# A hybrid encoder layer on one core: unit matrix ahead of the gram tiles, A queries ahead of A values, and other buffers for half of the output weight

## The chip, the core and the metric

The kernel runs on one core of a Trainium2 chip. The core has five engines with queues of their own: TensorE (PE, matrix products into PSUM), VectorE (DVE), ScalarE (ACT), GpSimd (POOL) and SyncE (SP, which here issues nearly all the DMAs). An engine works through its queue in order: an instruction that waits holds all that stand behind it on the same engine. The metric is the device time of one execution in microseconds; smaller is better. Matrix products are made of three matmuls with operands split into a high and a low part, so that the result is close to float32.

## What is computed

One layer of a streaming encoder on x of 1024 rows (tokens) by 1024 columns. Cut to its core:

```python
h = rms_norm(x, pre_norm_g)
proj = h @ w_in + b_in                       # 1024 x 3724, split by columns:
# a_q a_k a_v a_i a_f a_z | b_x b_z | c_r c_k c_v c_w c_a c_z | d_q d_k d_v d_f d_z
y_a = head_rms_norm(mlstm_chunkwise(silu(conv(a_q, a_k)), a_v, a_i, a_f)) * silu(a_z)
y_b = multiscale_pool(b_x) * silu(b_z)
y_c = rwkv7_time_mix(c_r, c_k, c_v, c_w, c_a, ...) * silu(c_z)
y_d = forgetting_attention(rms_norm(d_q), rms_norm(d_k), d_v, d_f) * silu(d_z)
y = concat(y_a, y_b, y_c, y_d) @ w_out
x = x + rms_norm(y, post_norm_g)
x = x + rms_norm(memory_cross_attention(rms_norm(x), rms_norm(mem), wq, wkv, wo))
```

Group C is a recurrence over tokens, S_t = S_{t-1}(diag(w_t) - kk^T (a*kk)) + v^T k. The kernel turns it into chunks of 64 tokens. Inside a chunk the recurrence is a triangular system, whose matrix has to be inverted; between chunks a state is passed on.

## The kernel before, in words

**Stages.** (1) The memory is normalised and its keys and values are computed; x is normalised and transposed. (2) The projections of group C (`cproj`) and their preparation (`cnorm`, `csplit`, `cprep`). (3) The gram tiles (`cgram`), the inverses (`cinv`, `tinv`) and the chain over 16 chunks (`cchain`). (4) Group A (`mpre`, `mlstm`) and group B. (5) Group D (`flog`, `ftr`, `fav`, `fin`) with the output projection (`wout`, `outproj`) beside it. (6) Cross attention.

**Order.** From stage 2 to the end of stage 5 PE's order is the order of the program text (`manual_schedule`). The queues of the other engines are put in order ahead of time by a planner, which takes instructions by their priority and by when it reckons that their inputs and buffers are ready; `high_priority` moves an instruction forward, `issue_after` holds it behind another one of the same engine. The orders are fixed when the kernel is built.

**Fillers.** The other projections are generators in a list, `fillers`. `fill(n)` takes n steps from the first of them, and when it is used up goes on to the next. One step of `tgemm` is three matmuls of 512 columns; `ngemm_q`, which the values use, counts a step as 0.5, with three matmuls of 268 or 256 columns. A generator writes its eviction when it is asked for the step after its last, so the fill after the 32nd step is the one in which the eviction of a `tgemm` of 32 steps enters the program. `ngemm_q` goes over the eight row blocks in groups of 2, 2 and 4 and keeps its four weight pieces to the last group; `tgemm` gives each piece back when its steps are done. The weight pieces go through the buffers "wr" (raw, two), "wh" and "wl" (four each). Results are put into "zu" (four buffers) on the way to DRAM. `rgemm` (the queries and keys) may carry norms of its results (`square`, `norm1`), which are put in after a number of filler steps.

**Preparation.** After the four `cnorm`, `fill(9)`, the tanh and split of the low-rank columns under `issue_after` of the last instruction named `act["cproj"]` so far, and `fill(5)` (L962 to L966). Then four groups of `cprep`, each followed by `fill(13)` and the second half of the group before it (L968 to L975), then `fill(4)`.

**Inverses.** `cgram` (L565) multiplies keys with queries of each chunk pair on PE; DVE masks one half into `bq`, ACT copies the other half back and POOL masks it (L581 to L585); sixteen DMAs write 32 by 32 blocks to the DRAM tile dN. `cinv` (L595) loads them with one DMA on ACT's queue, writes a unit matrix into `Tn` with two memsets on POOL (L599, L600) and inverts in 31 steps of two DVE instructions each (L604, L606). Result and transpose go to DRAM, and `tinv` (L611) reads them back in another layout; its first products on PE are L630. Between the loads and these products stands `fill(NI)`, NI = 46. The buffers "n4" (four of them) hold Nt and Tn, then the tiles of `tinv`, later the gate rows (`gaterows`, two of them) and the inputs of the convolution (`aconv`).

**Chain.** Each `cchain` takes three fills of two steps. After chunk c one piece of `gaterows` follows from c = 3 on, and one of `aconv` from c = 8 on. What is left of the fillers follows the chain (L1017).

**Output weight.** `wout(q)` (L1311) loads the 128 by 512 pieces k = 0 to 7 of the columns' half q, casts them on ACT and subtracts on POOL (k = 1, 4, 7) or DVE. Even pieces land in "wr", odd ones in "zu". `wout(0)` is called at the third step of group D (g = 2), `wout(1)` at the fifth, after which the buffers' pools are closed and the gain vector "gb" of the output projection is loaded into their room. The D gate (`zgemm(O_DZ, 3, True)`) is the filler at that time; its results go through "zu" too, and `tload` reads them from the DRAM tile zT for `tgate` and `fin`.

Of the kernel before, what the change touches and what calls it, by code (L numbers as in the profile page):

```python
# [36 lines left out]
def tile_trunk(ctx: ExitStack, tc: tile.TileContext, a, out, dbg=None):  # L37
# [63 lines left out]
    def wtile(kind, shape):  # L101
        dt = F32 if kind == "wr" else F32R
        n = wcount[kind]
        wcount[kind] += 1
        if cur["wp0"] is not None:
            a1, a0 = cur["wp"].tags[kind], cur["wp0"].tags[kind]
            if n % (a1 + a0) >= a1:
                return cur["wp0"](kind, shape, dt)
        return cur["wp"](kind, shape, dt)
# [285 lines left out]
    def fill(n):  # L395

        while n > 0 and fillers:
            try:
                w = next(fillers[0]) or 1
            except StopIteration:  # L400
                fillers.pop(0)
                continue
            n -= w
            for d in after:
                d[0] -= w
            for d in [d for d in after if d[0] <= 0]:
                after.remove(d)
                d[1]()
# [183 lines left out]
                    SY.dma_start(dN[q0:q0 + 8].rearrange("q s t -> s q t"),  # L592
                                 bq[r0:r0 + 32, cp * 2 - 2:cp * 2 + 2, :, r0:r0 + 32].rearrange("p c j t -> p (c j) t"))

    def cinv():  # L595
        Nt = cc("n4", [128, 32, 32])
        SC.dma_start(Nt, dN)
        Tn = cc("n4", [128, 32, 32])
        G.memset(Tn, 0.0)  # L599
        G.memset(Tn.rearrange("p a b -> p (a b)")[:, ::33], 1.0)  # L600
        for j in range(31):
            m = 31 - j
            pr = cc("pr", [128, m, j + 1])
            V.tensor_tensor(pr, Nt[:, j, j + 1:32][:, :, None].to_broadcast([128, m, j + 1]),  # L604
                            Tn[:, j, 0:j + 1][:, None, :].to_broadcast([128, m, j + 1]), op=ALU.mult)
            V.tensor_tensor(Tn[:, j + 1:32, 0:j + 1], Tn[:, j + 1:32, 0:j + 1], pr, op=ALU.add)  # L606
        V.tensor_copy(Nt, Tn.rearrange("p a b -> p b a"))
        SY.dma_start(dTt, Nt)
        SY.dma_start(dTn, Tn)
# [45 lines left out]
            SC.copy(SV[c - 1][0:64, 1::2, :], p[0:64, :, 64:128])  # L655

    FA, FB, FC = 2, 2, 2
    NI = 46
    BN = {}

    def cbk(c):
# [84 lines left out]
    def vgemm(wd, bias, c0, n, dst):  # L746
        ng = n - 256
        b = cm("bias", [128, 268])
        SY.dma_start(b[:, 0:n], bcast(bias[c0:c0 + n], n))

        zz = []

        def ev(i, p):
            if i % 2 == 0:
                zz.append(cur["stg"]("zu", [128, 2, 256]))
            z = zz[-1][:, i % 2, :]
            SC.copy(z, p[:, 0:256])
            if ng:
                SC.copy(gates[:, i, :], p[:, 256:n])  # L759
            if i % 2:  # L760
                V.tensor_tensor(zz[-1], zz[-1], b[:, None, 0:256].to_broadcast([128, 2, 256]), op=ALU.add)
                if ng:
                    g = gates[:, i - 1:i + 1, :]
                    V.tensor_tensor(g, g, b[:, None, 256:n].to_broadcast([128, 2, ng]), op=ALU.add)
                SY.dma_start(dst[(i - 1) * 128:(i + 1) * 128, :].rearrange("(a p) c -> p a c", a=2), zz[-1])
        yield from ngemm_q(wd, c0, n, hact, ev)
# [33 lines left out]
    def rgemm(c0, b0, r0, gcl=None, lag=None):  # L800
        us = []

        def put(t):
            c, hf = divmod(t, 2)
            SY.dma_start(rT[r0 + c * 128:r0 + (c + 1) * 128, hf * 512:(hf + 1) * 512], us[t])

        def square(t):
            sq = cur["stg"]("zt", [128, 512])
            SC.activation(sq, us[t], AF.Square)
            parts = [[cc(t_, [128, 256], F32R) for t_ in tags] for tags in (("bv", "yc"), ("ysb", "w"))]  # L810
            for q in range(2):
                qs = slice(q * 256, (q + 1) * 256)
                split_evac(parts[0][q], parts[1][q], sq[:, qs])
            defer(lag[t], lambda: norm(t, parts))

        def norm(t, parts):
            with tc.issue_after(act["ln"].ins):
                norm1(t, parts)

        def norm1(t, parts):  # L820
            p = ps("sm", [128, 512])
            for q in range(2):
                qs = slice(q * 256, (q + 1) * 256)
                T.matmul(p[:, qs], onesr, parts[0][q], start=True, stop=False)
                T.matmul(p[:, qs], onesr, parts[1][q], start=False, stop=True)
            if t < 3:
                square(t + 1)
            SC.activation(p, p, AF.Ln, bias=eps_n, scale=1.0 / 64)
            SC.activation(p, p, AF.Exp, scale=-0.5)
            V.scalar_tensor_tensor(us[t], us[t], col(gcl), p, op0=ALU.mult, op1=ALU.mult)  # L830
            put(t)

        def ev(c, p):
            for hf in range(2):
                u = cur["stg"]("zu", [128, 512])
                us.append(u)
                SC.activation(u, p[hf], AF.Identity, bias=col(b0 + c))
                if gcl is None:
                    put(2 * c + hf)
            if gcl is not None and c == 0:  # L840
                square(0)
        yield from tgemm(c0, 2, ev)
# [110 lines left out]
    with tc.manual_schedule(engines={PE}):  # L953
        run(cproj(6, 1))
        run(cproj(2, 2))
        fillers += [cproj(0, 2), cproj(4, 2), rgemm(O_DQ, 66, 0, 46, (7, 6, 6, 6))]
        gs = [cnorm(hf, j) for hf in range(2) for j in range(2)]
        for g in gs:
            next(g)
            fill(6)  # L960
            run(g)
        fill(9)  # L962
        with tc.issue_after(act["cnorm"].ins), tc.issue_after(act["cproj"].ins):
            SC.activation(shifted[6][0:64, :], shifted[6][0:64, :], AF.Tanh)
            csplit(0)
        fill(5)  # L966
        gs = [cprep(hf, j) for hf in range(2) for j in range(2)]
        for n, g in enumerate(gs):  # L968
            with tc.issue_after(act["cnorm"].ins):
                next(g)  # L970
            if g is gs[-1]:
                act["ln"] = tc.keep_in_program_order(SC.preload_act_table_set("natural_log_exp_and_others"))
            fill(13)
            if n:
                run(gs[n - 1])  # L975
        cur["vsplit"] = True
        fill(4)
        run(gs[-1])
        c1.close()
        fillers += [rgemm(O_DK, 68, 256, 47, (6, 6, 5, 5)), vgemm(a["w_av"], a["b_av"][0], 0, 268, avd), rgemm(O_AQ, 0, 512)]  # L980
        cc = Pool("cc", {"bq": 2, "n4": 4, "pr": 1, "t11": 1, "sv": 3, "ik": 2, "bn": 2, "w": 1, "uu": 1,
                         "bv": 1, "yc": 1, "ysb": 1})
        for _ in range(2):
            t = cc("ik", [128, 4, 64])
            for x in range(2):
                V.tensor_copy(t[PH[x], x::2, :], ident[PH[x], None, x * 64:(x + 1) * 64].to_broadcast([64, 2, 64]))
            IK.append(t)
        cprop(0)
        V.memset(SV[0][0:64, 0::2, :], 0.0)
        V.memset(SV[0][64:128, 1::2, :], 0.0)  # L990
        cgram(0, 1)
        cgram(1, 1)
        cinv()
        ti = [tinv(0), tinv(1)]
        next(ti[0])
        cur["vsplit"] = False
        fill(NI)
        next(ti[0])
        fill(4)
        run(ti[0])  # L1000
        fill(3)
        fillers += [rgemm(O_AK, 2, 768), vgemm(w_in, b_in, O_DV, 256, dvd)]
        gr, ac = gaterows(), aconv()
        tc.cur_priority = 150000
        cprop(1)
        cbk(0)
        for c in range(16):
            cchain(c)
            if c < 3:
                next(ti[1], None)  # L1010
            if c >= 3:
                next(gr, None)
            if c >= 8:
                next(ac, None)
        run(ac)
        cstore()
        while fillers:  # L1017
            fill(1)
# [292 lines left out]
    def wout(q):  # L1311
        for k4 in range(2):
            wh, wl = hT("h", [128, 4, 512], F32R), hT("l", [128, 4, 512], F32R)
            for x in range(4):
                k = 4 * k4 + x
                raw = cur["stg"]("zu", [128, 512]) if k % 2 else wtile("wr", [128, 512])
                SY.dma_start(raw, a["w_out"][0, k * 128:(k + 1) * 128, q * 512:(q + 1) * 512])
                woh[k, q], wol[k, q] = wh[:, x, :], wl[:, x, :]
                SC.copy(woh[k, q], raw)
                (G if k % 3 == 1 else V).tensor_tensor(wol[k, q], raw, f32(woh[k, q]), op=ALU.subtract)  # L1320
# [283 lines left out]
```

## Time and profile before

| | |
|---|---|
| Time, median of 3 runs | 950.1 us (949.56 to 950.68) |
| The profiled execution | 950.8 us, span 949.0 us |
| Mean granted clock of PE | 0.976 |
| VectorE busy | 543.8 us (57%) |
| ScalarE busy | 440.6 us (46%) |
| GpSimd busy | 221.5 us (23%) |
| HBM read, written | 83.92 MB, 28.87 MB |
| Gram tiles on PE begin | 203.9 us |
| Chain over chunks | 288 to 412 us |
| Group A and B | 412 to 542 us |
| Group D with the output projection | from 542 us |

The span reaches from the first to the last instruction; the time has some 1.8 us beside it. Lines such as L630 are those of the kernel before. A view of waits has the engine, the line that waited, for what it waited ("DMA t<-dTn" is a DMA into t from dTn), the sum in us, how often, and the longest. A timeline has the start, the duration, engine, line and operation, out<-in, shapes, and in brackets the idle time of the engine just before and what ended it; "x2" means that two like instructions are drawn as one row. A row of windows has the stretch, its length, busy us (and instructions) of PE, PEld, DVE, ACT and POOL, the granted clock (1.00 is full), the share of the DMA engines and GB/s. The rows of DMA issues have the queue, the count, KB each, and the median us from issue to landing.

### The profile page before, as it was taken

To read this page: it belongs to the slowest core of one execution; us is meant where nothing else is said; L and a number is where in the kernel's file an instruction comes from. 1 tells how busy PE (TensorE), PEld (TensorE's weight loads), DVE (VectorE), ACT (ScalarE), POOL (GpSimd) and SP (SyncE) were. 2 spreads that over 40 slices of the span, in tenths; PEclk is the share of its full clock that TensorE was granted. 3 is DMA by queue.
4 is the path that set the end of the run, shared out by engine and by line. 5 is a ranking of instruction groups with operands and counts; after the bars stand their busy time and mean duration, and the time that the engine had idled before them with its cause. 6 is when DMAs were issued, how large, how long until landed. Compare 5 with 4: busy or idle time off the path is not lost. (4 is left out here: it accounts for less than half of the span.)

```text
span 949.0 us, 16228 instructions
## 1 busy us (share of the span) xinstructions
PE 901.5 (95%) x6041; PEld 763.1 (80%) x6041; DVE 543.8 (57%) x1262; ACT 440.6 (46%) x1001; POOL 221.5 (23%) x243
## 2 busy tenths in 40 slices
PE   6999999899969999999999978999999999999997
PEld 6998887677858777987777756788887888889997
DVE  7684046876924348823895526665675455554225
ACT  7586166365524355624533334534464443444221
POOL 1012221139003335353333622000000000121211
PEclk9999999899959999999999999999999999999999
DMA  8877311112243131344754476532246301153104
GB/s 281 295 227 252 59 45 45 33 38 68 76 120 87 35 111 59 112 121 133 182 168 135 152 227 206 184 116 89 89 134 211 99 25 44 35 174 110 41 1 178
DMA packets 94432, 113.86 MB, mean 120 GB/s; under 512 B 21072, under 2 KB 68752, under 8 KB 94352
## 3 DMA queue, kind: packets, MB, share of 16 engines
q1 hardware_dynamic: 94064, 112.18, 38.4%
q8 instruction: 48, 0.79, 0.3%
q10 hardware_dynamic: 288, 0.63, 0.2%
q14 instruction: 32, 0.26, 0.1%
HBM read 83.92 MB, written 28.87 MB: 119 GB/s over the span
## 5 line engine op out<-in xcount | busy, mean ns | idle before, releaser
L137 PE MATMUL mm<-h,wh 128*128 128x512 f32 x528 | 220.5, 418 | 3.8 <-ACT zu L775 3.8
L139 PE MATMUL mm<-h,wl 128*128 128x512 f32 x528 | 210.6, 399 | 1.2 <-POOL wl L126 1.2
L138 PE MATMUL mm<-l,wh 128*128 128x512 f32 x528 | 210.7, 399 | 0.0
L126 POOL TENSOR_TENSOR wl<-wr,wh 128x512 fp32r<-128x512 f32 (+1 forms) x73 | 99.9, 1370 | 368.1 <-ACT wh L122 343.1
L137 PEld LDWEIGHTS mm<-h,wh 128*128 128x128 f32 x528 | 101.0, 191 | 29.4 <-ACT zu L775 4.6
L139 PEld LDWEIGHTS mm<-h,wl 128*128 128x128 f32 x528 | 101.0, 191 | 25.2 <-POOL wl L126 1.7
L138 PEld LDWEIGHTS mm<-l,wh 128*128 128x128 f32 x528 | 101.1, 191 | 18.2 <-issue 0.5
L122 ACT CAST wh<-wr 128x512 fp32r<-128x512 f32 (+1 forms) x122 | 74.4, 620 | 82.4 <-PE mm L138 38.5
L137 PE MATMUL mm<-wh,act 128*128 128x256 f32 x256 | 72.7, 284 | 0.0
L138 PE MATMUL mm<-wl,act 128*128 128x256 f32 x256 | 71.9, 281 | 0.0
L139 PE MATMUL mm<-wh,act 128*128 128x256 f32 x256 | 71.8, 281 | 0.0
L137 PE MATMUL mm<-h,act 128*128 128x512 f32 x128 | 53.6, 419 | 0.3 <-ACT jk L1338 0.3
L139 PE MATMUL mm<-h,act 128*128 128x512 f32 x128 | 50.5, 394 | 0.0
L138 PE MATMUL mm<-l,act 128*128 128x512 f32 x128 | 50.1, 392 | 0.0
L137 PEld LDWEIGHTS mm<-wh,act 128*128 128x128 f32 x256 | 48.2, 188 | 0.1
L138 PEld LDWEIGHTS mm<-wl,act 128*128 128x128 f32 x256 | 48.3, 189 | 0.0
L139 PEld LDWEIGHTS mm<-wh,act 128*128 128x128 f32 x256 | 48.2, 188 | 0.0
L137 PE MATMUL mm<-mT,wh 128*128 128x256 f32 x128 | 37.3, 291 | 8.7 <-ACT wh L122 8.7
L137 PE MATMUL mm<-wh,h 128*128 128x268 f32 (+1 forms) x128 | 40.2, 314 | 3.8 <-ACT gates L759 3.8
L1529 DVE TENSOR_TENSOR o<-mm,gb 128x256 f32<-128x256 f32 x32 | 13.6, 425 | 43.8 <-ACT junk L1528 43.5
L1475 ACT ACTIVATE e<-lgp,tf,r 128x256 f32<-128x256 f32 x32 | 18.1, 565 | 43.5 <-DVE tf L1472 43.5
L138 PE MATMUL mm<-wl,h 128*128 128x268 f32 (+1 forms) x128 | 37.9, 296 | 0.0
(404 smaller groups left out, 2006.8 us busy)
## 6 DMA issues: line engine op xcount, KB each, us to landing
wr<-in_w_in_dram SPq DMA_DIRECT2D x54, 256.0 KB, 2.8
wr<-in_wkv_dram SPq DMA_DIRECT2D x32, 256.0 KB, 4.2
x<-in_x_dram SPq DMA_DIRECT2D x16, 512.0 KB, 5.3
x<-x1d SPq DMA_DIRECT2D x15, 512.0 KB, 5.5
wr<-in_xattn_wo_dram SPq DMA_DIRECT2D x16, 256.0 KB, 3.1
vwd<-row SPq DMA_DIRECT2D x8, 512.0 KB, 3.9
rT<-zu SPq DMA_DIRECT2D x16, 256.0 KB, 2.1
u<-rT SPq DMA_DIRECT2D x16, 256.0 KB, 4.5
```

The costliest lines, as they stand in the source:

```text
L122: SC.copy(hi, raw)
L126: G.tensor_tensor(lo, raw, f32(hi), op=ALU.subtract)
L137: T.matmul(o, lh, rh, start=st, stop=False, skip_group_check=skip)
L138: T.matmul(o, lh, rl, start=False, stop=False, skip_group_check=skip)
L139: T.matmul(o, ll, rh, start=False, stop=sp, skip_group_check=skip)
L1475: SC.activation(e, p, AF.Exp, bias=nb, scale=r2[:, i:i + 1], accum_out=dn)
L1529: V.tensor_tensor(o3[i][:, gs], p, xog[:, gs], op=ALU.mult)
```

## The change

Four edits in one. The unit matrix is written by a new function `tunit`, called ahead of the two `cgram`, and handed to `cinv`. The fills of the preparation go from 9, then 13 four times, then 4 to 7, then 13 and 14 three times, then 3 (the same sum), and NI from 46 to 50. The A queries stand ahead of the A values in the list of fillers, and the gate rows, which need the gates that come with the values, begin after chunk 7. In the first half of the output weight all eight pieces use the two "wr" buffers; the second half is as before.

```diff
-    def cinv():
-        Nt = cc("n4", [128, 32, 32])
-        SC.dma_start(Nt, dN)
+    def tunit():
         Tn = cc("n4", [128, 32, 32])
         G.memset(Tn, 0.0)
         G.memset(Tn.rearrange("p a b -> p (a b)")[:, ::33], 1.0)
+        return Tn
+
+    def cinv(Tn):
+        Nt = cc("n4", [128, 32, 32])
+        SC.dma_start(Nt, dN)
...
-    NI = 46
+    NI = 50
...
-        fill(9)
+        fill(7)
...
-            fill(13)
+            fill(14 if n else 13)
...
-        fill(4)
+        fill(3)
         run(gs[-1])
         c1.close()
-        fillers += [rgemm(O_DK, 68, 256, 47, (6, 6, 5, 5)), vgemm(a["w_av"], a["b_av"][0], 0, 268, avd), rgemm(O_AQ, 0, 512)]
+        fillers += [rgemm(O_DK, 68, 256, 47, (6, 6, 5, 5)), rgemm(O_AQ, 0, 512), vgemm(a["w_av"], a["b_av"][0], 0, 268, avd)]
...
+        tn = tunit()
         cgram(0, 1)
         cgram(1, 1)
-        cinv()
+        cinv(tn)
...
-            if c >= 3:
+            if c >= 7:
                 next(gr, None)
...
-                raw = cur["stg"]("zu", [128, 512]) if k % 2 else wtile("wr", [128, 512])
+                raw = cur["stg"]("zu", [128, 512]) if k % 2 and q else wtile("wr", [128, 512])
```

## The prediction

> **What bounds the kernel now.** I read the shares of the page first, then TensorE's waits, then windows around the largest waits, then the queues of the engines that those waits name.
>
> ```profile
> span 949.0 us, 16228 instructions
> PE 901.5 (95%) x6041; PEld 763.1 (80%) x6041; DVE 543.8 (57%) x1262; ACT 440.6 (46%) x1001; POOL 221.5 (23%) x243
> PE sm L630 <- DMA t<-dTn: 7.0, 1, 7.0
> PE mm L137 <- ACT zu L775: 3.8, 1, 3.8
> PE mm L137 <- ACT gates L759: 3.8, 2, 3.0
> PE tr L1303 <- DVE zt L1244: 3.7, 1, 3.7
> PE sm L137 <- ACT gc L530: 2.6, 1, 2.6
> PE sm L825 <- DVE ysb L161: 2.4, 1, 2.4
> ```
>
> TensorE (PE) is busy 95% of the span, so a change that removes no matmul can only win back waits and the slow clock behind them. The six waits listed are 23.3 us, and the change stands next to all six. Three rows of them lie in one place, around the inverses (on a norm, on evictions, on the inverse itself), which the windows show.
>
> ```profile
> 233.31:267.80 34.49, 28.23 (x166) 25.32 (x165) 32.47 (x83) 15.18 (x34) 4.77 (x5) 0.87 0.30 100
> 267.80:274.76 6.96, 0.01 (x1) 0.03 (x1) 0.00 (x0) 0.62 (x1) 2.30 (x3) 0.50 0.63 199
> 274.76:288.21 13.45, 13.45 (x174) 13.20 (x175) 2.12 (x3) 3.02 (x5) 1.27 (x1) 0.70 0.23 38
> 288.21:412.20 123.99, 123.76 (x1249) 102.73 (x1248) 69.31 (x171) 61.91 (x192) 46.95 (x54) 0.99 0.27 81
> ```
>
> After the times stand PE, PEld, DVE, ACT and POOL busy, then the granted clock. From 233.31 to 267.80 it is VectorE (DVE) that is full, 32.47 of 34.49 us: it computes the inverses (L604, L606) with PE on fillers. Then PE stands still for 6.96 us until L630 has the inverse back from DRAM. From 288.21 to 412.20 the chunk chain runs with PE busy 123.76 of 123.99 us: there every filler matmul lengthens the stage. So before 274.76 the end of the inverse decides, and after 288.21 the work left for PE.
>
> **The change part by part. First, the unit matrix and the filler order.**
>
> ```profile
> 227.81 1.51 DVE L161 TENSOR_TENSOR w<-zt,yc 128x256 fp32r<-128x256 f32 x1
> 233.51 0.19 DVE L604 TENSOR_TENSOR pr<-n,n 128x31 f32<-128x31 f32 x1 [4.19 <-POOL n L600]
> 235.88 1.32 DVE L606 TENSOR_TENSOR n<-n,pr 128x87 f32<-128x87 f32 x1
> 264.74 0.24 DVE L606 TENSOR_TENSOR n<-n,pr 128x87 f32<-128x87 f32 x1
> 207.31 2.62 POOL L585 TENSOR_TENSOR t<-t,maskG 64x512 f32<-64x512 f32 x2 [7.40 <-ACT t L584]
> 219.36 11.11 POOL L585 TENSOR_TENSOR ee<-ee,maskG 64x512 f32<-64x512 f32 x8
> 225.69 0.34 ACTq L597 DMA_DIRECT2D n<-dN  x1
> n<-dN ACTq DMA_DIRECT2D x1, 512.0 KB, 3.2
> ```
>
> The first inverse step waits 4.19 us for the memset L600 on GpSimd (POOL), which sits behind eight mask products of 11.11 us. The two memsets are only moved: ahead of the gram tiles they fall into POOL's idle 7.40 us before 207.31, so I cost them at nothing there; should the freed memory of the closed pool come late, they delay those masks by about their own length, and the masks have no waiter on the path. The other input, the loaded Nt, lands at 225.69 + 3.2 = 228.9, and DVE is taken until 227.81 + 1.51 = 229.3. The start moves from 233.5 to 229.3: **-4.2 us**. It then runs while POOL is still at its masks: 1.32 against 0.24 us for the same 87 elements shows what a small step can cost beside POOL, so I give back **+0.8** (one such step; bounds 0 and four of them, 4.3, the whole gain).
>
> ```profile
> L761 DVE TENSOR_TENSOR zu<-zu,bias 128x512 f32<-128x512 f32 x2 | 1.4, 684 | 0.0
> 266.59 0.38 SPq L609 DMA_DIRECT2D dTn<-n  x1
> 269.88 0.38 SPq L115 DMA_DIRECT2D wr<-in_w_in_dram  x1
> 270.86 1.49 SPq L618 DMA_DIRECT2D t<-dTn  x2
> dTn<-n SPq DMA_DIRECT2D x1, 512.0 KB, 2.9
> t<-dTn SPq DMA_DIRECT2D x4, 64.0 KB, 3.5
> ```
>
> With the A queries (512 columns, evicted at their end) ahead of the A values (evicted after each two row blocks), the bias additions leave the inverse's stretch: **-1.4** on DVE. From the inverse to L630 there are a store, 2.9, and two loads, 3.5 each, on SyncE's (SP's) queue. The store was issued at 266.59 and landed near 269.5; a weight load for the queries stood ahead until 269.88 because its buffers were held by the values, which keep all four weight pieces to their last group. The queries give pieces back as they go, so up to 1.4 us may go; a load for the next gemm may stand there instead, so I take **-0.5** (bounds -1.4 and +2). Together L630 moves from 274.8 to 269.5 (-5.3).
>
> ```profile
> 185.01 0.40 PE L137 MATMUL mm<-h,wh 128*128 128x512 f32 x1
> 185.71 0.40 PE L137 MATMUL mm<-h,wh 128*128 128x512 f32 x1
> 246.56 0.29 PE L137 MATMUL mm<-wh,h 128*128 128x268 f32 x1
> 246.94 0.29 PE L137 MATMUL mm<-wh,h 128*128 128x268 f32 x1
> ```
>
> A query step is 185.71 - 185.01 = 0.70 us; a value step 0.38, and two of them count as one of NI. Before, NI = 46 took 26 steps of the D keys and 20 value units, 20 x 0.75 = 15.0 us. Now 50 is 26 and 24 query steps, 16.8 us: **-1.8** of work that the full chain no longer does. The value steps run by 246.56, so 24 query steps in their place end by about 264, ahead of 269.5; the waits on L759 and on L161 disappear into the wait for L630, now 5 us or more; what is late next is still the inverse. The slow clock behind that wait (0.70 mean to 288.21) I leave as it is. The values now come in the chain: the gate rows wait for them, hence chunk 7 instead of 3, and the one query step and 32 value units left there end, at 6 a chunk, in chunk 5. Site sum: -5.3 - 1.8 = **-7.1**.
>
> **Second, the fills of the preparation.**
>
> ```profile
> 174.87 0.69 ACT L530 ACTIVATE gc<-sm,pc 128x512 f32<-128x512 f32 x1 [2.26 <-DVE bk L554]
> 238.00:242.00 4.00, 3.98 (x11) 3.10 (x12) 3.76 (x12) 1.70 (x3) 0.00 (x0) 0.57 0.36 131
> 258.00:262.00 4.00, 1.59 (x11) 1.27 (x10) 3.86 (x12) 3.11 (x9) 0.00 (x0) 1.00 0.16 56
> ```
>
> fill(9) to fill(7) leaves the 32nd step of cproj(0,2) untraced when issue_after names its instruction, so the tanh and split of the low-rank columns need not queue behind that eviction on ScalarE (ACT), and the first group comes two steps, 1.4 us, earlier. The third group's wait of 2.64 us is ACT waiting for DVE to free gc at 174.87; DVE's run starts up to 1.4 us earlier, and PE arrives 13 + 14 steps later instead of 13 + 13, net 0.7 earlier. So the wait falls by 0.7 to 1.4; I take **-1.0**. Bounds: +1.4, two steps, if the eviction now stands behind tanh and split and its PSUM comes late; -4.3 if the whole wait goes, and with it a half clock, 4 x 0.43 = 1.7 by the row at 238. Everything to the inverse hangs behind this, so it adds.
>
> On that clock, the rows: after the 2.40 us wait for L161 it was 0.57, around the 0.87 us wait at 259 it was 1.00. [...]
>
> **Third, the output weight.**
>
> ```profile
> 548.87 0.33 SPq L1317 DMA_DIRECT2D wr<-in_w_out_dram  x1
> 551.98 0.62 ACT L1319 CAST h<-wr 128x512 fp32r<-128x512 f32 x1 [7.21 <-DMA wr<-in_w_out_dram]
> 575.30 0.33 SPq L1317 DMA_DIRECT2D wr<-in_w_out_dram  x1
> 588.40 0.35 SPq L155 DMA_DIRECT2D gb<-in_post_norm_g_dram  x1
> gb<-in_post_norm_g_dram SPq DMA_DIRECT2D x1, 512.0 KB, 4.2
> 594.20 0.50 PE L137 MATMUL mm<-h,act 128*128 128x512 f32 x1 [0.33 <-ACT jk L1338]
> ```
>
> The odd pieces of the first half take the two "wr" buffers instead of "zu", so eight loads follow one another where four did, and the D gate's eviction meets free "zu". Behind a load that waits on SP stand the rows of tload and of the next mask; behind its cast on ACT the exponentials and evictions. That eviction (L775) was late because ACT stood 7.21 us at a cast whose load came at 548.87, and VectorE's queue behind the same piece. The second piece is now k = 1, whose subtraction goes to POOL, not DVE, which frees DVE and then the exponentials by up to 1.6 us, while its load still waits for the same weight buffer. I take **-1.0** of the 3.8 and leave the wait on L1244. Bounds: -10 if both waits of 3.8 and 3.7 and the slow clock behind them go; +10 by the rival below.
>
> Sum: -7.1 - 1.0 - 1.0 = **-9.1**. The profiled execution took 950.8 us, span 949.0, 0.7 above the median of 950.1; from the median it is 950.1 - 9.1 = **941.0 us**.
>
> **Rivals.** *More goes* (0.17): the earlier wait goes whole (3.3 more) and so does one wait at the output weight (3.7 + 1.7 - 1.0 = 4.4): 933.3. For it: one eviction and one free queue are enough. Against: static orders that merely swap which piece blocks.
>
> *The inverse gains little* (0.17): the memsets go early as written, but DVE's order puts norm work first, POOL takes the 4.3, or SP holds the store behind a weight load (+2); then little but the 1.8, the 1.0 or so remains: 947. That the change doesn't do what it says would be this too: the memsets kept late by a buffer, 4.2 less.
>
> *The loads of the output weight become the bound* (0.06): seven loads from 548.87 to 575.30 went at 26.4 / 6 = 4.4 us each. Twelve on two buffers, eleven from 548.87 on, end at 593; the last cast and the gain vector, issued at 588.40 and 4.2 us long, slip by some 9. The eviction for which PE already waits 0.33 us at 594.20 is as late: +9, +10 with the clock, 951, within 0.2%. Against: the first buffer is free before 548.87, so two loads can go at once, and the "zu" loads of the second half no longer wait for the D gate.
>
> *Slower* (0.10): gate rows in chunks 7 to 12 keep two of the four "n4" buffers where the convolution (chunks 8 to 15) had them, so its loads come one after the other.
>
> ```profile
> n<-rT SPq DMA_DIRECT2D x4, 512.0 KB, 3.4
> ```
>
> Where a convolution step stands in DVE's order ahead of the chain's small copies, each load of 3.4 us holds the chain and PE with it; a pair of filler steps covers 1.4. Four loads with waits and slow clock cost 4 x (2.0 + 1.7) = 14.8: 956. It decides from the point where a load lands more than 1.4 us behind its place in the queue; against it, DVE has half of the chain's time idle.
>
> **How the numbers follow.** Forecast 0.50 (936.5 to 945), more 0.17, little 0.17 (945 to 948.5), loads 0.06, slower 0.10. The predicted time is 941.0. The range for 8 in 10 is 931.5 to 949.0: it takes in the first three cases but the far end of the second, and leaves out the last two. About 0.2%, 1.9 us, can be told from no change here; faster takes the first two and nearly all of the third, 0.83, the same 0.07, slower 0.10.
>
> **What would show it.** L604 starts 4 us nearer to the load of Nt and names no POOL; a wait at L630 remains, between 4 and 9 us, with no wait on L759 or L161 before it; behind the chain one filler unit is left instead of five; the wait on L530 shrinks. Wrong would be a wait of 7 us or more with the inverse ending as long after its start and as late as before, a PE wait inside the chain (it had 0.23 us), or "gb" issued later after the D gate than now.

## The result, and the profile after

| | before | after |
|---|---|---|
| Time, median | 951.86 us (949.56 to 955.82, 10 runs) | 959.95 us (955.12 to 963.85, 10 runs) |
| Ratio, 95% interval | | 1.0072 (1.0044 to 1.0099): slower |
| Profiled execution | 950.8, span 949.0 | 955.53, span 953.7 |
| First gram matmul on PE | 203.9 | 208.3 |
| First inverse step on DVE | 233.5 | 233.6 |
| First matmul of L630 (after: L633) | 274.8 | 275.0 |
| First chunk's first chain matmul, L679 (L682) | 288.6 | 287.2 |
| From there to the same matmul of the last chunk | 116.7 | 124.7 |
| Last matmul | 942.4 | 946.9 |

The forecast was 941.0; the kernel became slower. The new function shifts the lines behind it by 3 (by 4 from the end of the chain on), so L630 is L633 here, L679 is L682. Of the changed kernel's runs, those near 955 us were granted a mean clock of 0.980 to 0.984 and those above 960 us 0.973 to 0.975; the profiled execution is of the first kind, so it shows 4.7 us of a loss whose median is 8.1.

The first lines of the changed kernel's page, and TensorE's waits over its whole span (without the one at the start of the kernel, 8.9 us, which was 8.7 before):

```profile
span 953.7 us, 16219 instructions
PE 901.1 (94%) x6041; PEld 760.9 (80%) x6041; DVE 544.7 (57%) x1262; ACT 439.6 (46%) x1001; POOL 222.3 (23%) x243
```

```profile
PE sm L633 <- DMA t<-dTn: 6.3, 1, 6.3
PE mm L137 <- ACT zu L778: 3.8, 2, 3.5
PE cs L696 <- DVE w L684: 3.4, 3, 1.5
...
PE mm L137 <- ACT jk L1342: 2.4, 1, 2.4
PE sm L137 <- DVE bon L560: 2.0, 1, 2.0
PE tr L1307 <- DVE zt L1248: 1.9, 1, 1.9
```

PE is busy for the same 901 us as before, on the same 6041 matmuls: what changed is waiting. The wait on L759 went (3.8 to nothing), that on L1244 shrank (3.7 to 1.9), and the one at the inverse (L633) is 0.7 shorter. The wait of 2.0 us that ends with L560 is the third group's, which was 2.6 and ended with L530. The waits on the copy w (L684) and on L1342 came up or grew, the first of them in the chain, which had almost none. Over the whole span the clock is no part of this loss: the trace has 31.0 us at half clock (a mean clock of 0.984), that of before 44.9 (0.976). Windows over the same four stretches as those shown of before:

```profile
233.38:269.20 35.82, 32.34 (x143) 24.92 (x141) 34.21 (x80) 19.38 (x38) 10.40 (x9) 1.00 0.30 91
269.20:275.02 5.82, 0.00 (x1) 0.03 (x1) 1.62 (x2) 0.00 (x0) 3.14 (x3) 0.63 0.98 302
275.02:287.21 12.19, 12.19 (x153) 10.54 (x154) 1.37 (x2) 2.76 (x5) 0.00 (x0) 0.76 0.29 84
287.21:416.00 128.79, 122.38 (x1299) 105.88 (x1298) 69.82 (x171) 61.67 (x195) 46.56 (x53) 0.99 0.25 74
```

The chain (last row) left PE 6.4 us without work, where it had 0.23; POOL is busy 10.40 us beside the inverse (first row), where it had 4.77. So three places answer: the preparation lost 4.4 us ahead of the gram tiles, the inverse site won 5.8 behind them (84.7 to 78.9 us from the first gram matmul to the chain), and the chain lost 8.0. Behind the chain 2 us come back.

Of the chain's 8.0 us, 5.8 are waits of PE between the two matmuls. The rest, some 2 us, is work that stands in another place. From the first to the last chunk the chain takes 90 filler units in either kernel. Counted by their matmuls, before they were 64 query steps and 26 units of values (two value steps each); now they are 33 and 57. At the prediction's 0.70 and 0.75 us that is 1.6 us more, an estimate, and about as much came back behind the chain.

### The profile page after: what moved, and what is told of

It reads as the page before. It is cut to its first block, busy times and chain, and to the rows that moved or that the text cites. A ratio compares the mean times of both kernels' runs of the same rounds, so it can differ in the third digit from the quotient of the medians.

```text
span 953.7 us, 16219 instructions
## 1 busy us (share of the span) xinstructions
PE 901.1 (94%) x6041; PEld 760.9 (80%) x6041; DVE 544.7 (57%) x1262; ACT 439.6 (46%) x1001; POOL 222.3 (23%) x243
## 5 line engine op out<-in xcount | busy, mean ns | idle before, releaser
L139 PE MATMUL mm<-mT,wl 128*128 128x256 f32 x128 | 37.4, 292 | 0.1
```

Of the source, the lines that this page charges most:

```text
L139: T.matmul(o, ll, rh, start=False, stop=sp, skip_group_check=skip)
```

## The experiments

Theory at this point: the gate rows, late as they now are, meet the convolution in DVE's queue and hold the chain; the fills cost the preparation; the unit matrix wins; the output weight does nothing. Each part was therefore made alone first. Kernels without the unit matrix keep the line numbers of before; those with it have the shifted ones. "Gram" is the time of the first gram matmul, "chain" the time from the first to the last chunk's first chain matmul, both in the profiled execution.

| kernel | median us | ratio to before (95%) | gram | L630/L633 | chain |
|---|---|---|---|---|---|
| unit matrix alone | 949.08 | 0.9972 (0.9960 to 0.9984) | 203.8 | 272.4 | 115.1 |
| fills alone | 955.45 | 1.0031 (1.0017 to 1.0046) | 209.2 | 278.9 | 116.7 |
| order alone | 958.29 | 1.0077 (1.0059 to 1.0094) | 204.0 | 272.7 | 127.5 |
| output weight alone | 953.94 | 1.0029 (1.0016 to 1.0041) | 203.4 | 274.1 | 116.8 |
| gate rows from chunk 7 alone | 959.87 | 1.0087 (1.0072 to 1.0101) | 203.3 | 274.5 | 123.7 |
| order, convolution held back | 951.50 | 0.9992 (0.9979 to 1.0006) | 204.1 | 272.8 | 119.5 |
| order, gate rows twice a chunk | 955.52 | 1.0045 (1.0029 to 1.0061) | 204.5 | 273.4 | 125.1 |
| fills of 14 alone | 957.04 | 1.0060 (1.0038 to 1.0082) | 208.1 | 279.1 | 122.3 |
| fill of 7 alone | 952.28 | 0.9998 (0.9983 to 1.0014) | 203.0 | 270.1 | 117.7 |
| output weight, low parts on DVE | 951.69 | 1.0004 (0.9994 to 1.0015) | 204.6 | 274.9 | 116.9 |
| unit matrix, NI = 50 | 950.07 | 0.9989 (0.9979 to 1.0000) | 204.0 | 272.6 | 118.1 |
| unit matrix, fills 13, 16, 15, 8 | 950.19 | 0.9990 (0.9977 to 1.0004) | 202.6 | 271.2 | 116.8 |
| unit matrix, both of these | 951.62 | 1.0007 (0.9993 to 1.0021) | 205.7 | 274.7 | 120.6 |
| the change once more | 961.45 | 1.0088 (1.0057 to 1.0119) | 207.0 | 273.7 | 124.7 |
| the change without its order part | 955.91 | 1.0042 (1.0028 to 1.0057) | 208.4 | 276.8 | 115.1 |
| the change without its fills | 956.83 | 1.0057 (1.0039 to 1.0075) | 203.9 | 270.5 | 126.1 |

### The four parts, one at a time

**Unit matrix.** Edit, on the kernel before:

```diff
+        tn = tunit()
         cgram(0, 1)
         cgram(1, 1)
-        cinv()
+        cinv(tn)
```

> Before with one part of the change alone: the unit matrix is written ahead of the gram tiles; fills, order of the fillers, gate rows and output weight as before. Theory (the step was sized right, the loss lies elsewhere): the inverse starts 4 us nearer to the gram tiles and the end moves with it, 3 to 4 us under the kernel before. Rival (what the earlier start wins is lost inside the inverse to small copies that run beside POOL's tensor_tensor, which took 1.2 to 1.5 us each in the changed kernel): within 1 us of the kernel before, with the inverse's stretch 2 us or more longer than 33.0 us.

Measured 949.08, ratio 0.9972: 2.8 us faster, a little less than the theory's 3 to 4. DVE in the changed kernel, and POOL beside it:

```profile
233.58 1.28 DVE L607 TENSOR_TENSOR pr<-n,n 128x31 f32<-128x31 f32 x1
234.90 1.24 DVE L609 TENSOR_TENSOR n<-n,pr 128x31 f32<-128x31 f32 x1
236.18 0.22 DVE L607 TENSOR_TENSOR pr<-n,n 128x60 f32<-128x60 f32 x1
```

```profile
232.01 2.80 POOL L585 TENSOR_TENSOR ee<-ee,maskG 64x512 f32<-64x512 f32 x2
234.78 1.29 POOL L126 TENSOR_TENSOR wl<-wr,wh 128x512 fp32r<-128x512 f32 x1
```

The first step no longer names POOL and comes 25.3 us behind the first gram matmul instead of 29.6, which is the 4.2 of the forecast. But the first two steps, of 31 elements, take 1.28 and 1.24 us while POOL works, where the first step took 0.19; the third is back at 0.22. In the run with this edit alone the inverse grew from 33.0 to 34.9 us, so of 4.3 us 2.4 are left at its end and 2.3 at the first product behind it. The theory's total is the nearer one, but the rival's mechanism is there: the start gains 4, the longer inverse takes nearly 2 of it.

**Fills.** Edit, on the kernel before:

```diff
-        fill(9)
+        fill(7)
...
-            fill(13)
+            fill(14 if n else 13)
...
-        fill(4)
+        fill(3)
         run(gs[-1])
```

> Before with the four new sizes of the preparation's fills alone (7 for 9, 14 for 13 three times, 3 for 4). Theory: the first gram tile comes 4 us later (208 against 203.9 us), because the table load and the tanh stand ahead of the evictions that TensorE waits for, and because two or three waits near 2 us leave stretches at a lower clock; the whole is 4 us slower, 955 to 956. Rival (the fills only move work between two places, and what the preparation loses the chain or the inverse's cover gets back): within 1 us of the kernel before though the first gram tile is 4 us later.

Measured 955.45, ratio 1.0031, gram at 209.2: the theory's loss, paid to the end. TensorE's waits of this kernel in the preparation, and windows (stretch, length, PE busy, granted clock, DMA share, GB/s):

```profile
147.35 0.50 PE L137 MATMUL mm<-h,wh 128*128 128x512 f32 x1 [1.67 <-DVE rk L485]
175.13 0.79 PE L137 MATMUL sm<-sp,lora 64*128 64x512 f32 x1 [2.05 <-DVE bon L560]
191.17 0.79 PE L137 MATMUL sm<-sp,lora 64*128 64x512 f32 x1 [0.83 <-ACT gc L530]
```

```profile
184.00:190.00 6.00, 6.00 (x32) 1.00 0.18 44
190.00:198.00 8.00, 7.17 (x17) 0.57 0.01 2
198.00:209.00 11.00, 11.00 (x58) 1.00 0.19 49
```

The third group's wait fell from 2.64 to 2.05, by 0.6 where the forecast reckoned 0.7 to 1.4, and it now ends with L560 on DVE. New are 1.67 us at 147 and 0.83 us at 191, and behind the latter a stretch at 0.57 in which 17 matmuls ran, where the kernel before ran 35 in the same 8 us at a clock of 1.00.

**Order.** Edit, on the kernel before:

```diff
-    NI = 46
+    NI = 50
...
-        fillers += [rgemm(O_DK, 68, 256, 47, (6, 6, 5, 5)), vgemm(a["w_av"], a["b_av"][0], 0, 268, avd), rgemm(O_AQ, 0, 512)]
+        fillers += [rgemm(O_DK, 68, 256, 47, (6, 6, 5, 5)), rgemm(O_AQ, 0, 512), vgemm(a["w_av"], a["b_av"][0], 0, 268, avd)]
...
-            if c >= 3:
+            if c >= 7:
                 next(gr, None)
```

> Before with the order alone: A queries pending ahead of A values, 50 units in place of 46 ahead of the inverse's limit, and the gate rows from chunk 7 in place of chunk 3. Theory (the gate rows fall together with the convolution in chunks 8 to 15 and VectorE's queue holds the chain's small copies): the last chunk's first chain matmul comes 6 us later or more, 956 to 958 us. Rival (the gate rows are free where they are, and the order alone gains at the inverse): 949 to 951 us.

Measured 958.29, ratio 1.0077; L630 comes 2.1 us earlier, the chain starts 3.3 earlier and its last chunk 7.5 later (10.8 us longer). As the theory had it, and the rival falls. Of the 10.8 us, 7.0 are waits, 1.7 is one more stretch of 3.4 us at half clock, and the rest is the exchange of filler units.

**Output weight.** Edit, on the kernel before:

```diff
-                raw = cur["stg"]("zu", [128, 512]) if k % 2 else wtile("wr", [128, 512])
+                raw = cur["stg"]("zu", [128, 512]) if k % 2 and q else wtile("wr", [128, 512])
```

> Before with the first half of the output weight through two buffers alone. Theory: nothing on the path, within 0.8 us of the kernel before, with the stage from the first favour matmul to the last as long as before. Rival (the wait of 2.41 us on the line that makes the gate's product in the changed kernel belongs to this edit): 2 us slower or more.

Measured 953.94, ratio 1.0029: here the theory falls, the edit is not free. TensorE, SP and DVE of this kernel in group D:

```profile
570.00 0.41 PE L1303 MATMUL tr<-cst,rE 128*128 128x128 f32 x2 [0.88 <-DVE zt L1244]
575.09 0.47 PE L137 MATMUL mm<-h,act 128*128 128x512 f32 x1 [1.67 <-DVE zu L773]
582.21 0.44 PE L1280 MATMUL tr<-cst,lg 128*128 128x128 f32 x2 [2.28 <-ACT lg L1270]
596.49 0.50 PE L137 MATMUL mm<-h,act 128*128 128x512 f32 x1 [1.58 <-ACT jk L1338]
```

```profile
590.72 0.35 SPq L155 DMA_DIRECT2D gb<-in_post_norm_g_dram  x1
```

```profile
595.02 0.69 DVE L1337 TENSOR_TENSOR y<-mm,gb 128x512 f32<-128x512 f32 x1 [1.70 <-DMA gb<-in_post_norm_g_dram]
```

The wait on L1244 falls from 3.73 to 0.88, and 1.67, 2.28 and 1.58 take its place. The last begins with "gb", issued 2.3 us later than before (588.40), because the second half's last piece is subtracted later and its buffer gives "gb" its room. The eviction of the first output tile waits for it, and PE for the eviction.

### Why the late gate rows cost 7 us

**Gate rows alone.** Edit, on the kernel before:

```diff
-            if c >= 3:
+            if c >= 7:
                 next(gr, None)
```

> Before with the gate rows alone moved from chunk 3 to chunk 7; A values still ahead of A queries, 46 units. Theory (the loss of the order run is the meeting of gate rows and convolution in chunks 8 to 12): from the first to the last chunk's first chain matmul 10 us longer than the 116.7 us of the kernel before, whole 957 us or more. Rival (the loss comes from the A values, which now stand with their evictions and bias adds inside the chain): within 1.5 us of the kernel before.

Measured 959.87, ratio 1.0087; the chain takes 123.7, against 127.5 with the whole order part. The theory named 126.7 and 957 or more; the rival falls, since A values stand where they stood. VectorE of this kernel in chunk 10, and the matmul that waits for L681 (the copy w of the chain; the row with "..." leaves out seven scans of some 0.15 us):

```profile
369.25 0.24 DVE L894 COPY n<-sm 1x96 f32<-1x96 f32 x1
369.42 0.40 DVE L726 TENSOR_TENSOR yc<-ysb,tc 128x256 f32<-128x256 f32 x1
369.75 1.23 DVE L898 TENSOR_TENSOR_SCAN n<-n 1x8 f32<-1x8 f32 x1
...
371.48 0.40 DVE L730 TENSOR_REDUCE tc<-pr 128x4 f32<-128x256 f32 x1
371.81 0.17 DVE L900 TENSOR_TENSOR n<-n 1x32 f32<-1x32 f32 x1
371.91 0.73 DVE L944 SCALAR_TENSOR_TENSOR t<-n,pc,t 128x512 f32<-128x512 f32 x1
372.57 0.16 DVE L901 TENSOR_SCALAR n<-n 1x32 f32<-1x32 f32 x1
372.65 0.40 DVE L681 COPY w<-cw 128x256 f32<-128x256 f32 x1
```

```profile
373.11 0.45 PE L693 MATMUL cs<-w,n 64*64 64x64 f32 x8 [2.63 <-DVE w L681]
```

Gate rows (L894 to L901), the convolution (L944) and the norm of the chunk before (L726, L730) stand in one row ahead of one copy of 0.40 us, and PE waits 2.63 us for it. DVE is not short of time over the chain (busy for 69.31 of its 123.99 us before); the copy stands in the wrong place of an order fixed ahead.

Not all of the 2.63 us is the order. The first scan took 1.23 us where the seven behind it took some 0.15, and POOL was at work beside it:

```profile
369.51 1.44 POOL L126 TENSOR_TENSOR wl<-wr,wh 128x512 fp32r<-128x512 f32 x1 [0.21 <-ACT wh L122]
```

In the changed kernel DVE has the same row of work in chunk 10 with no POOL instruction beside the scans; there all eight took some 0.15 us, and PE waited 1.54 us. So about 1.1 of the 2.63 us (2.63 - 1.54, an estimate) belongs to the slow scan. Of the 7.0 us that this run's chain is longer, 5.1 are waits and 1.7 one more stretch of 3.4 us at half clock.

**Convolution out of the way.** Edit, on the order kernel:

```diff
-            if c >= 8:
+            if c >= 14:
                 next(ac, None)
```

> The order run (A queries first, 50 units, gate rows from chunk 7) with the convolution held back to chunk 14, so that the two no longer meet; what is left of it runs behind the last chunk. Theory: the chain takes 117 us again as in the kernel before, in place of 127.5; the convolution behind it is paid later, so the whole says little (950 to 960). Rival (A values inside the chain cost): the chain stays at 124 us or more.

Measured 951.50, ratio 0.9992: with the same late gate rows and the same order, all of the order part's loss is gone. The chain takes 119.5, not the 117 of the theory, but below the 124 of the rival: 1.2 of the 2.8 us that are left are waits, the rest is the exchange of filler units. So the loss needs both, gate rows and convolution in the same chunks.

**Gate rows earlier.** Edit, on the order kernel; `mid` is called in `cchain` behind `fill(FB)`:

```diff
+        def mid(c):
+            if 7 <= c < 10:
+                next(gr, None)
...
-            if c >= 7:
+            if c >= 6:
                 next(gr, None)
```

> The order run with the gate rows as early as the A values allow and twice a chunk: one step behind chunk 6, then one in the middle and one at the end of chunks 7 to 9, so that four of the six steps come before chunk 9. Theory: the meeting is shorter, the chain takes 119 to 123 us, the whole 951 to 954. Rival (each step of the gate rows costs the same wherever it stands in the second half): as the order run, 957 to 959.

Measured 955.52, between the theory's 951 to 954 and the rival's 957 to 959; the chain takes 125.1, outside what the theory gave (119 to 123). ScalarE, VectorE and TensorE of this kernel at the place that lost most (its lines behind the middle of `cchain` stand one later, so L703 is the chain's new state, L702 before):

```profile
383.99 1.33 ACT L942 ACTIVATE t<-n,pc 128x512 f32<-128x512 f32 x2 [3.58 <-DMA n<-rT]
```

```profile
384.74 1.42 DVE L945 SCALAR_TENSOR_TENSOR t<-n,pc,t 128x511 f32<-128x511 f32 x2 [3.82 <-ACT t L942]
386.07 0.60 DVE L703 TENSOR_TENSOR sv<-cs,eg 64x128 f32<-64x128 f32 x2
```

```profile
386.49 1.73 PE L679 MATMUL cw<-sv,ee 128*128 128x64 f32 x7 [3.08 <-DVE sv L703]
```

It is a load of the convolution that is late: ACT stands 3.58 us for it, DVE behind ACT, the chain's new state behind DVE, and PE waits 3.08 us. So the loads matter by themselves. In the changed kernel the four loads (SP) and the last of ACT's waits for them read:

```profile
358.79 0.38 SPq L942 DMA_DIRECT2D n<-rT  x1
379.88 0.38 SPq L942 DMA_DIRECT2D n<-rT  x1
386.20 0.32 SPq L942 DMA_DIRECT2D n<-rT  x1
396.21 0.32 SPq L942 DMA_DIRECT2D n<-rT  x1
```

```profile
399.83 0.72 ACT L944 ACTIVATE t<-n,pc 128x512 f32<-128x512 f32 x1 [4.69 <-DMA n<-rT]
```

Before, the trace has them at 350.19, 354.31, 381.25 and 387.50. The second comes 21 us behind the first where it came 4 behind it, and the longest wait of SP for such a load ends with a matmul of the gate rows, L915:

```profile
SPq L942 <- PE sm L915: 5.4, 1, 5.4
```

The gate rows hold two "n4" buffers, the loads have one left, and the convolution slides to the end of the chain.

### The fills: which one, and what the clock does

**The fills of 14 alone**, on the kernel before (the sum is then two steps more):

```diff
-            fill(13)
+            fill(14 if n else 13)
...
-        fill(4)
+        fill(3)
         run(gs[-1])
```

> Before with the fills of 14 for 13 three times and 3 for 4, the fill of 9 kept. Theory (the cost of the fills run is the wait of 0.83 us on the column L530 at 191 us and the half clock behind it, which hangs on how the 14 stand against ACT's work): first gram tile 4 us later as in the fills run, 954 to 956 us. Rival (it is the fill of 7, which puts the table load ahead of the evictions and makes ACT late from there on): first gram tile within 1 us of the kernel before's 203.9, 951 to 952.5 us.

**The fill of 7 alone**, on the kernel before (the sum is then two steps less):

```diff
-        fill(9)
+        fill(7)
```

> Before with the fill of 9 made 7 alone, so that two units fewer stand in the preparation and two more behind it. Theory (the run with the fills of 14 alone lost 4 us at the first gram tile by itself, so the fill of 7 is not needed for the loss): first gram tile within 1.5 us of 203.9, the whole within 1.5 us of the kernel before. Rival (table load and tanh ahead of the evictions cost by themselves): a wait of 1.5 us or more near 146 us and a whole 2 us or more slower.

The fills of 14 gave 957.04 and gram at 208.1, the fill of 7 952.28 and gram at 203.0: the loss ahead of the gram tiles comes with the 14. The two steps more and the two steps less are 1.4 us of work by themselves, which leaves 2.8 us lost with the 14 and 0.5 with the 7. The fill of 7 does have its wait of 1.66 us at 148 for the eviction that now stands behind table load and tanh, as its rival said, but the whole is as before. TensorE of the kernel with the 14, its clock, and ScalarE's queue later in the chain:

```profile
173.64 0.58 PE L137 MATMUL mm<-h,wh 128*128 128x512 f32 x1 [2.14 <-DVE v L485]
178.97 0.79 PE L137 MATMUL sm<-sp,lora 64*128 64x512 f32 x1 [0.83 <-ACT gc L530]
```

```profile
170.50:173.92 3.42, 1.28 (x6) 1.00 0.29 75
173.92:184.16 10.24, 9.41 (x26) 0.50 0.09 26
```

```profile
388.75 1.34 ACT L941 ACTIVATE t<-n,pc 128x512 f32<-128x512 f32 x2 [3.66 <-DMA n<-rT]
390.09 0.53 ACT L711 COPY ysb<-cw 64x128 f32<-64x128 f32 x2
```

The loss is the theory's, its place is not: here one wait of 2.14 us at 173 has 10.2 us at half clock behind it, where before has 6.8 there, and the wait at 191 is not there; the 0.83 us on L530 comes at 179, while the clock is already at half. And the chain, of which this edit touches nothing, is 5.6 us longer: the convolution's product L941 now stands ahead of the chain's copy L711 in ACT's order, waits 3.66 us for its load, and PE waits 2.34 us for the copy. In the kernel before L711 stood ahead, and ACT waited 0.65 us for the load.

**More cover for the third group.** Edit, on the unit matrix kernel:

```diff
-            fill(13)
+            fill((13, 16, 15, 8)[n])
```

> Before with the unit matrix ahead and the four fills of 13 made 13, 16, 15 and 8 (the same total), so that three units more stand ahead of the third group. Theory (a wait of over 2 us there leaves TensorE at half clock for 5 us, both of which more cover takes away): no wait and no half clock at 173 to 181 us, the first gram tile at 200 to 202 us in place of 203.9, the whole 945 to 947.5. Rival (VectorE's work on the four groups is the limit of this stage, so that the wait comes up one group later): first gram tile at 203.5 to 205 us, the whole 948.5 to 950.

Measured 950.19, on the rival's side. The clock was 1.00 from 170 to 202 us, as the theory said, but PE waits come back elsewhere (2.10 us at 173 on L485, 1.58 at 201 on L560) and the gram tiles come 1.3 us earlier only.

**Four more units at the inverse.** Edit, on the unit matrix kernel:

```diff
-    NI = 46
+    NI = 50
```

> Before with the unit matrix ahead and 50 units in place of 46 ahead of the inverse's limit; A values still ahead of A queries, gate rows from chunk 3. Theory (what the order part gains at the inverse comes from the four units more, not from the exchange, and the gate rows can stay): the chain takes 115 to 117 us, the whole 945 to 947.5, that is 2 us or more under the run with the unit matrix alone (949.1). Rival (units taken from the chain are missed there): as that run, 948.5 to 950.

Measured 950.07, beside the rival's range. The wait at L633 does fall from 7.0 to 4.2 us, but the chain takes 118.1 in place of 115.1, with 2.0 us of waits on its copy L698.

**Both.** The two edits together, on the unit matrix kernel:

```diff
-    NI = 46
+    NI = 50
...
-            fill(13)
+            fill((13, 16, 15, 8)[n])
```

> Unit matrix ahead, 50 units, and fills of 13, 16, 15 and 8 together. Theory: what the two runs with one of them gain beyond the unit matrix adds up, 942 to 945 us. Rival (each of them moves other engines' work against the chain or the output stage and loses there): 947 to 950.

Measured 951.62 with a chain of 120.6: slower than either foresaw; the gains don't add, as the rival had it.

### The output weight's buffers

All low parts of the first half go to DVE. Edit, on the output weight kernel:

```diff
-                (G if k % 3 == 1 else V).tensor_tensor(wol[k, q], raw, f32(woh[k, q]), op=ALU.subtract)
+                (G if k % 3 == 1 and q else V).tensor_tensor(wol[k, q], raw, f32(woh[k, q]), op=ALU.subtract)
```

> The output weight run (first half through two buffers) with all eight low parts of that first half on VectorE in place of five there and three on POOL. Theory (a buffer is held until the low part is made, and POOL's took 1.55 us beside 0.69 on VectorE, so that loads, casts and what stands behind the casts on ScalarE come late): half or more of the 2 us that the edit cost goes, 951.5 to 953. Rival (the loads themselves are the limit, two at a time): as that run, 953.5 to 955.

Measured 951.69, ratio 1.0004: as the theory said, the loss is gone. SP and TensorE of this kernel:

```profile
587.52 0.34 SPq L155 DMA_DIRECT2D gb<-in_post_norm_g_dram  x1
```

```profile
593.30 0.50 PE L137 MATMUL mm<-h,act 128*128 128x512 f32 x1 [0.31 <-ACT jk L1338]
```

"gb" goes out 3.2 us earlier than with the parts on POOL, and the wait at the first output tile is 0.31 instead of 1.58. So the twelve loads on two buffers are not the limit, and the rival falls. That POOL's longer hold on a buffer was the cause fits (in the output weight kernel the first half's three took 1.26 to 1.46 us there, one of DVE's on the same buffers 0.68); the edit also takes the parts out of POOL's queue, which this run cannot tell apart.

### The parts inside the whole

The changed kernel was run once more as it is, then with its order part taken back, then with its fills taken back:

```diff
-    NI = 50
+    NI = 46
...
-        fillers += [rgemm(O_DK, 68, 256, 47, (6, 6, 5, 5)), rgemm(O_AQ, 0, 512), vgemm(a["w_av"], a["b_av"][0], 0, 268, avd)]
+        fillers += [rgemm(O_DK, 68, 256, 47, (6, 6, 5, 5)), vgemm(a["w_av"], a["b_av"][0], 0, 268, avd), rgemm(O_AQ, 0, 512)]
...
-            if c >= 7:
+            if c >= 3:
                 next(gr, None)
```

```diff
-        fill(7)
+        fill(9)
...
-            fill(14 if n else 13)
+            fill(13)
...
-        fill(3)
+        fill(4)
         run(gs[-1])
```

> The changed kernel once more, as the measure for the next two on the same chip. Both theories: 956 to 961 us, ratio 1.005 to 1.009.

> The changed kernel with the order part taken back: A values ahead of A queries, 46 units, gate rows from chunk 3; unit matrix, fills and output weight as in the change. Theory (the order part, with its late gate rows, makes the sign): 6 us or more under the changed kernel, 950 to 953.5 us, the chain 115 to 118 us. Rival (the fills make it): 954 us or more.

> The changed kernel with the fills of the kernel before; unit matrix, order and output weight as in the change. Theory (the order part makes the sign and the fills add 2 to 3 us): 955 to 958 us, first gram tile at 204 us, the chain still 123 us or more. Rival (the fills make the sign): 952 us or less.

961.45, 955.91 and 956.83. Without the order part the chain is 115.1, as the theory said, but the whole is 955.91, in the rival's range; without the fills it is 956.83, in the theory's. So no single part makes the sign: taking back the order gains 0.46 points, the fills 0.31, and either rest is still slower than the kernel before. The parts alone sum to -0.28 + 0.31 + 0.77 + 0.29 = 1.09 points, the whole measured 0.72 and 0.88, with intervals that reach from 0.44 to 1.19. The best of all versions run is the unit matrix alone, 0.28% faster than the kernel before.

## Why the prediction was wrong, step by step

**The unit matrix.** Start -4.2: measured -4.3 behind the gram tiles, and no POOL named, as it was to show. The +0.8 for contention was mis-sized: the inverse became 2.5 us longer in the changed kernel and 1.9 with the edit alone, within the bounds of 0 to 4.3.

**Bias additions -1.4, SP -0.5, work moved -1.8.** The order run's inverse was no shorter (33.4 against 33.0), so the bias additions gave nothing. From the inverse's end to L630 it saved 2.45 us (8.29 to 5.84), more than the 0.5 taken: the weight load no longer stands on SP between the two stores. Another 1.2 came to the chain's start. The work moved ahead did come back, 2.0 us behind the chain, but the sum left out that the chain takes a fixed number of units and now has the longer ones (some 1.6 us). The site as a whole won 5.8 where -7.1 was forecast: right in kind.

**The preparation -1.0.** The third group's wait shrank by 0.6, a little less than worked out. The sum left out that more steps ahead of a group also shift ACT's and DVE's queues against the following groups. New waits of 0.83 to 2.1 us came up, which end with DVE and ACT (that the shift made them is argued from this, no run shows it apart), and the stage has 10.2 us at half clock where it had 6.8: +4.4 measured, beyond the bound of +1.4. That bound's mechanism, the eviction behind tanh and split, did occur (1.66 us) and cost nothing in the end; the fills of 14 did.

**The output weight -1.0.** The wait on L1244, which the forecast left as it was, shrank (3.73 to 0.88 with the edit alone); the one on L775 stayed (3.83 to 3.64). The step "which frees DVE" counted the subtraction that goes to POOL as a gain; the edit lost 2.8 us by the ratio, and moving the first half's low parts from POOL to DVE took the loss away. The rival *loads* had the sign to look for right, the later "gb", with 9 us of delay where 2.3 came, but not its cause: the same twelve loads on the same two buffers cost nothing once DVE made the low parts.

**The chain, forecast at no loss, is the step that failed and that made the wrong sign with the preparation.** The text put the gate rows into chunks 7 to 12 at no cost and gave the rival *slower* 0.10, because "DVE has half of the chain's time idle". That share is true after the change too (69.82 of 128.79 us busy) and decides nothing: one copy of some 0.4 us in the wrong place stopped PE for 1.5 us at a time in the changed kernel, and for 2.63 with the gate rows alone. The rival's mechanism was the right one: "n4" buffers held by the gate rows, loads late, small copies held in DVE's order. That its 956 lies near the measured 960 (955.5 in the profiled execution) is luck: it set 14.8 us for the chain, which lost 8.0, against 9.1 us of gains elsewhere, of which 3.4 came. The sign to look for, a PE wait inside the chain, was named and came: 6.4 us.

How the clock followed the waits can be read from the traces. In those of the kernel before and of the changed kernel the granted clock, from its first record at 13.2 and 14.8 us on, changes only at points that lie whole multiples of 3.41 us apart, and counted from the start of the span these points lie elsewhere in the two: the first is 173.66 us in one and 175.18 in the other. Two waits of nearly one length on the same line, L485, were followed by different clocks. The 2.14 us in the kernel with the 14 (shown above) lay whole in the 3.41 us ahead of a change at 173.92, and PE was busy for 37% of the stretch; half clock followed. The 2.10 us in the kernel with the fills 13, 16, 15 and 8 fell into two such stretches, counted back in steps of 3.41 us from that kernel's next change at 203.5:

```profile
169.34:172.75 3.41, 1.71 (x8) 1.00 0.30 77
172.75:176.17 3.42, 3.02 (x17) 1.00 0.29 77
```

PE was busy for 50% and 88% of the two stretches, and the clock stayed at 1.00. In the traces of the kernel before and of the changed kernel, 9 stretches at full clock have PE busy for less than half of their 3.41 us, and 8 of them were followed by half clock; of the 518 others, 5 were. The wait of 0.83 us at 191 in the changed kernel is among the five: its stretch was 76% busy. In another of them, 303.36 to 306.78 us before, PE was busy throughout. What decided in these five is not shown.

Left open: what the 3.4 us are by which the median loss exceeds that of the profiled execution, since only one execution of each kernel has a trace; and by what rule the planner put the convolution ahead of the chain's copy in a kernel whose chain was not edited. Where the unit matrix kernel loses part of its gain can be read from its trace: it is 4.2 us ahead at the end of the chain and level at the last matmul, and between the two it has 17.1 us at half clock where before has 6.8. Its median is 2.8 us ahead.

## What to carry to other kernels

A mean idle share of an engine says little about moving work into a stage whose critical chain passes through that engine by small instructions: look at what the fixed order puts ahead of each of them, and at which loads those stand behind. Split a bundle of edits and time each part; here one of four won, and the three others hid it. Where TensorE is 95% busy, work moved earlier only helps if the waits that it displaces do not come back elsewhere, with a half clock behind them (here 10.2 us of it in the preparation, where before had 6.8).

## What the hardware showed unexpectedly

The same wait of 0.83 us at L530 was followed by different stretches at half clock: by 3.4 us from 192.2 on in the changed kernel, by 6.8 us from 191.2 in the fills kernel and from 190.5 in the change without its order part; before, a wait of 0.87 us that ended at 259.0 was followed by 3.4 us at 1.00, though PE was busy for 74% of its stretch and not 76%, and half clock came at 262.4, behind a stretch 43% busy. And two VectorE steps on 31 elements per partition that began beside a POOL tensor_tensor took 1.28 and 1.24 us in the changed kernel (POOL's took 1.36 and 1.29) and 1.34 and 1.25 with the unit matrix alone, where they took 0.19 and 0.21 before; with the gate rows from chunk 7 alone, a scan of 8 elements took 1.23 us beside one of 1.44, and 0.15 without.
